# A ninth column in the first heads' inverse root, and k's second half sent from ScalarE's queue

## The chip, the cores and the metric

One NeuronCore of a Trainium2 chip runs the whole program once. The metric is the device time of that execution in microseconds (us); lower is better. The core has five engines that run side by side, each with its own in-order instruction stream: TensorE (PE: matmuls; its weight loads are shown as PEld), VectorE (DVE), ScalarE (ACT), GpSimd (POOL) and SyncE (SP), which here only starts transfers. ScalarE can start transfers too; a transfer is then an instruction of its stream, and it waits there for its data like any other.

## The reference, cut to what matters

Two transformer layers over 512 tokens of width 1024. Layer 0 mixes with eight dilated-window heads (A) and eight sliding-window heads (B), layer 1 with sixteen forgetting-attention heads (C); each layer ends in a squared-ReLU MLP. What the change touches is at the start of layer 0 and in every head:

```
h = rms_norm(x, g_mix)                  # per token: x * rsqrt(mean(x*x) + EPS) * g
proj = h @ w_in
q = rms_norm(q per head, q_gain)        # per token and head of 64 columns
k = rms_norm(k per head, k_gain)
scores = q @ k.T * scale + bias         # then softmax, times v
```

## The kernel before, in words

Tokens lie in four tiles of 128. The projections run on the transposed input, multiplied by the gain but not yet by the tokens' inverse root. That root is put in afterwards: v is multiplied by it when it leaves PSUM (`rcol`, one column per token tile, in `prep_v`), and for q and k, which are normed per head anyway, only its EPS term is needed (`ecol`, added in `norm_heads`). Every matrix product is made of three fp32r products (high x high, low x high, high x low), so each weight tile `wraw` is split into `whi` (ScalarE or GpSimd) and `wlo` (VectorE or GpSimd), and each activation into a high and a low half.

`start` does the first projection (q and k of the first four A heads, `pj`) while its inputs arrive: for each of eight chunks of 128 input columns it splits the input chunk (`h`, high on ScalarE, low on VectorE) and the weight chunk, and issues twelve matmuls. Between chunks it squares the tokens (`junk`, `ms`, chunks 3 to 6) and makes tables for the attention biases. After chunk 6 it calls `col_stats`: two small operations give `msv` and `ecol`, and eleven dependent ones in `rsqrt_small` (a shift, a subtraction and three Newton rounds of three) give `rcol`. In `start` these are held in program order, ahead of chunk 7's low halves. Then `use(outs)` calls `norm_heads`: copies of `pj` to `qk` and squares on ScalarE, sums `ss` on VectorE, `ssv`, the same eleven operations over 32 columns (8 heads in 4 tiles), and four multiplications of `qk`, two on VectorE and two on GpSimd.

Next comes the v projection of these heads (`v_a(0)`), then attention, interleaved with further projections as filler for TensorE. Per pair of heads `prep_q` and `prep_k` transpose `qk` on TensorE, split it, and `prep_k` copies the 64 partitions of each k to the other 64 by a transfer from SBUF to SBUF (256 KB in reads and writes, 26 of them in all), since the score matmul takes high and low from both halves. Weight and bias loads share SyncE's queue with these transfers, in program order.

Outside the places held in program order, a scheduler fixes the order on each engine when the program is built. PSUM has four banks in `pA` (projections) and four in `pB` (transposes, scores, outputs); the v projection may write a bank only when the q,k projection in it was copied out, and the next projection (k and v of B, `kv_b`) only when `prep_v` has read v.

Of the kernel before, what the change touches and what calls it, by code (L numbers as in the profile page):

```python
# [9 lines left out]
F32 = mybir.dt.float32  # L10
F32R = mybir.dt.float32r
BF16 = mybir.dt.bfloat16
I32 = mybir.dt.int32
AF = mybir.ActivationFunctionType
OP = mybir.AluOpType
# [3 lines left out]
P = 128  # L19
# [50 lines left out]
def trunk(ctx, tc, x, b_sinks, w_out_even, b_forget, w_out_odd, w_up, w_down, xt, gains, w_in_even, w_in_odd, out):  # L70
# [46 lines left out]

    cnt = {"hi": 0, "start": False}

    def rsqrt_small(dst, v):  # L120

        n = v.shape[2]
        y, t1 = (small.tile([P, NT * 8], F32, tag=f"rsq{i}", name="rsq")[:, :NT * n]
                 .rearrange("p (t h) -> p t h", h=n) for i in range(2))
        b = small.tile([P, NT * 8], I32, tag="rsqb", name="rsqb")[:, :NT * n].rearrange("p (t h) -> p t h", h=n)
        in_order(nc.vector.tensor_scalar(b, v.bitcast(I32), 1, None, op0=OP.logical_shift_right))
        in_order(nc.vector.tensor_scalar(y.bitcast(I32), b, -1.0, float(0x5f3759df), op0=OP.mult, op1=OP.add))
        for k in range(3):
            in_order(nc.vector.scalar_tensor_tensor(t1, v, -0.5, y, op0=OP.mult, op1=OP.mult))
            in_order(nc.vector.tensor_mul(t1, t1, y))  # L130
            in_order(nc.vector.scalar_tensor_tensor(dst if k == 2 else y, t1, 1.5, y, op0=OP.add, op1=OP.mult))
# [8 lines left out]
    def in_order(m):  # L140
        if cnt["start"]:
            tc.keep_in_program_order(m)
# [50 lines left out]
    def layer_attention(li, hT, w_in, w_out, stats=None):  # L193


        with ExitStack() as c2:
# [39 lines left out]
                use(outs)  # L236
                yield 0

            def norm_heads(outs, nh, sq_tag="sq", sq_bufs=1 + li):

                w = nh * HD
                qk = [ap.tile([P, 2, 512], F32, tag="qk", bufs=4, name="qk") for _ in range(2)]
                ss = small.tile([P, NT, 8], F32, tag="ss", name="ss")
                for t in range(NT):
                    nc.scalar.copy(qk[t // 2][:, t % 2, :w], outs[t][:, :w])
                for t in range(NT):
                    q = qk[t // 2][:, t % 2, :w]
                    sq = ap.tile([P, 512], F32, tag=sq_tag, bufs=sq_bufs, name="sq")
                    nc.scalar.activation(sq[:, :w], q, AF.Square)
                    nc.vector.reduce_sum(ss[:, t, :nh], sq[:, :w].rearrange("p (h d) -> p h d", d=HD), axis=AX.X)  # L250
                v = small.tile([P, NT, 8], F32, tag="ssv", name="ssv")
                for t in range(NT):
                    nc.vector.tensor_scalar(v[:, t, :nh], ss[:, t, :nh], 1.0 / HD, ecol[:, t:t + 1],
                                            op0=OP.mult, op1=OP.add)
                rs = small.tile([P, NT, 8], F32, tag="rs", name="rs")
                rsqrt_small(rs[:, :, :nh], v[:, :, :nh])
                for t in range(NT):
                    q = qk[t // 2][:, t % 2, :w].rearrange("p (h d) -> p h d", d=HD)
                    eng = nc.gpsimd if NORM[t] == "g" else nc.vector
                    eng.tensor_mul(q, q, rs[:, t, :nh].unsqueeze(2).to_broadcast([P, nh, HD]))  # L260
                return qk

            def head_T(qk, off):
# [17 lines left out]
            def prep_k(qk, off, g):  # L281

                pt = head_T(qk, off)
                ks = []
                for h in range(2):
                    k = ap.tile([P, 2, 512], F32R, tag="K", bufs=3, name="K")
                    r = slice(h * HD, (h + 1) * HD)
                    r2 = slice((1 - h) * HD, (2 - h) * HD)
                    scale_split(k[r, 0], k[r, 1], pt[r], g[r])
                    nc.sync.dma_start(k[r2].bitcast(F32), k[r].bitcast(F32))  # L290
                    ks.append(k)
                return ks

# [204 lines left out]
                return use  # L498

            def qk_use(key, nh, *sq):  # L500
                def use(outs):
                    st["qk", key] = norm_heads(outs, nh, *sq)
                return use

            def all_of(gen):
# [91 lines left out]
    def start(ap, hT, w_in, tables, outs, use):  # L597

        w = bank("pB", "warm")
        for _ in range(WARM):
            nc.tensor.matmul(w[:, :P], identb, identb, start=True, stop=True)

        cnt["start"] = True
        xs = [ap.tile([P, 2, 512], F32, tag="qk", bufs=4, name="xs") for _ in range(4)]
        raws = [wp.tile([P, 2, 512], F32, tag="wraw", bufs=RAW, name="wraw") for _ in range(4)]
        tok = [acc_slot(f"x{i}") for i in range(4)]

        def load(what, k, n):  # L610
            if what == "t":
                dst = tok[k]
                src = x[0, k % 2 * 256:k % 2 * 256 + 256, k // 2 * 512:k // 2 * 512 + 512]
            else:
                dst = (xs if what == "x" else raws)[k // 2][:, k % 2:k % 2 + n]
                src = (xt if what == "x" else w_in[:, :512])[k * P:(k + n) * P]
            in_order(nc.sync.dma_start(dst, src.rearrange("(c p) t -> p c t", p=P)))

        for what, k, n in (("x", 0, 1), ("w", 0, 1), ("x", 1, 1), ("w", 1, 1), ("x", 2, 2), ("w", 2, 2), ("t", 0, 0), ("x", 4, 2),
                           ("t", 1, 0), ("w", 4, 2), ("t", 2, 0), ("x", 6, 2), ("t", 3, 0), ("w", 6, 2)):  # L620
            load(what, k, n)
        ms = small.tile([P, 2, NT], F32, tag="ms0", name="ms0")
        sink = small.tile([P, HA], F32, tag="sink", name="sink")
        for _ in range(TABLES0):
            next(tables)
        for k in range(DC):
            g = gcol[:, k:k + 1]
            src = xs[k // 2][:, k % 2]
            h = slot(f"h0_{k}")
            hT.append(h)  # L630
            hi = wp.tile([P, 512], F32R, tag="whi", bufs=NHI, name="whi")
            lo = wp.tile([P, 512], F32R, tag="wlo", bufs=NLO, name="wlo")
            raw = raws[k // 2][:, k % 2]
            if k == 0:
                in_order(nc.scalar.activation(h[:, 0, :256], src[:, :256], AF.Copy, scale=g))
                in_order(nc.scalar.copy(hi, raw))
                in_order(nc.scalar.activation(h[:, 0, 256:], src[:, 256:], AF.Copy, scale=g))
                in_order(nc.vector.tensor_sub(lo, raw, hi.bitcast(F32)))
                in_order(nc.vector.scalar_tensor_tensor(h[:, 1], src, g, h[:, 0].bitcast(F32), op0=OP.mult, op1=OP.subtract))
            else:  # L640
                scale_split(h[:, 0], h[:, 1], src, g)
                split(hi, lo, raw, "act")
            products = ((0, hi), (0, lo), (1, hi))
            for n, (t, i) in enumerate([(t, i) for i in range(3) for t in range(NT)] if k == 0 else
                                       [(t, i) for t in range(NT) for i in range(3)]):
                part, wt = products[i]
                m = nc.tensor.matmul(outs[t], h[:, part, t * P:(t + 1) * P], wt, start=k == 0 and i == 0,
                                     stop=k == DC - 1 and i == 2)
                if k == 0:
                    in_order(m)  # L650
            for _ in range(TABLES[k]):
                next(tables)
            if k == 1:
                in_order(nc.scalar.dma_start(sink, bass.AP(tensor=b_sinks.tensor, offset=b_sinks.offset, ap=[[0, P], [1, HA]])))
                in_order(nc.scalar.dma_start(bfor, bass.AP(tensor=b_forget.tensor, offset=b_forget.offset, ap=[[0, P], [1, HC]])))
            if 3 <= k < 7:
                i = k - 3
                for t in range(2):
                    junk = ap.tile([P, 512], F32, tag="sq", bufs=1, name="junk")
                    in_order(nc.scalar.activation(junk, tok[i][:, t], AF.Square,  # L660
                                                  accum_out=ms[:, i // 2, i % 2 * 2 + t:i % 2 * 2 + t + 1]))
            if k == 6:
                in_order(nc.vector.tensor_add(ms[:, 0], ms[:, 0], ms[:, 1]))
                col_stats(ms[:, 0])
        cnt["start"] = False
        nc.gpsimd.tensor_scalar(nsink, sink, -1.0, 1.0, op0=OP.mult, op1=OP.mult)
        tc.keep_in_program_order(nc.vector.tensor_mul(gg, gcol[:, 32:38:2], gcol[:, 33:38:2]))
        use(outs)
        for _ in tables:
            pass  # L670

# [586 lines left out]
```

## Time and profile before

| what | us |
|---|---|
| median of 3 runs (1164.63 to 1164.91) | 1164.66 |
| the profiled execution | 1165.4 |
| its span | 1163.6 |
| TensorE busy in the span | 1144.3 |
| VectorE / ScalarE / GpSimd busy | 875.7 / 646.4 / 201.1 |

The profiled execution's time lies 1.8 us above its span and 0.7 us above the median. Of the 1163.6 us, TensorE is not busy in 19.3; where it is busy without a break, a stage is as long as its matmuls. In lists of waits the columns are: who waited and on which line, for whom, us in total, times, longest. In the timeline: start, duration, engine, line, operation, and in brackets the idle time before it with what ended it.

### The profile page before, as it was taken

To read this page: it belongs to the slowest core of one execution; us is meant where nothing else is said; L and a number is where in the kernel's file an instruction comes from. 1 tells how busy PE (TensorE), PEld (TensorE's weight loads), DVE (VectorE), ACT (ScalarE), POOL (GpSimd) and SP (SyncE) were. 2 spreads that over 40 slices of the span, in tenths; PEclk is the share of its full clock that TensorE was granted. 3 is DMA by queue.
4 is the path that set the end of the run, shared out by engine and by line. 5 is a ranking of instruction groups with operands and counts; after the bars stand their busy time and mean duration, and the time that the engine had idled before them with its cause. 6 is when DMAs were issued, how large, how long until landed. Compare 5 with 4: busy or idle time off the path is not lost.

```text
span 1163.6 us, 17370 instructions
## 1 busy us (share of the span) xinstructions
PE 1144.3 (98%) x6228; PEld 979.7 (84%) x6228; DVE 875.7 (75%) x1875; ACT 646.4 (56%) x1342; POOL 201.1 (17%) x292
## 2 busy tenths in 40 slices
PE   8999999999999999999999999999999999999998
PEld 6887887888988988988887888888888888888887
DVE  7877999968868857855646877778858759669676
ACT  6455867656545545444235685656756455465452
POOL 0345534100000000000255445332100000000000
PEclk9999999999999999999999999999999999999999
DMA  7432124142332333333443323343420721623403
GB/s 272 145 83 81 37 50 150 56 127 88 95 109 91 93 107 92 108 111 110 146 128 109 110 84 108 101 131 114 164 99 8 233 86 56 198 73 110 146 35 109
DMA packets 94694, 126.56 MB, mean 109 GB/s; under 512 B 5888, under 2 KB 66304, under 8 KB 94608
## 3 DMA queue, kind: packets, MB, share of 16 engines
q1 hardware_dynamic: 93568, 123.29, 34.4%
q10 hardware_dynamic: 1040, 2.16, 0.5%
q8 instruction: 49, 0.80, 0.3%
q14 instruction: 37, 0.30, 0.1%
HBM read 114.39 MB, written 4.23 MB: 102 GB/s over the span
## 4 chain that ended last, share of the span: by engine, by line
PE 87%; DVE 5%; DMA 3%; ACT 2%; issue 1%; POOL 1%; SPq 0%; POOLq 0%; DVEq 0%; ACTq 0%
PE up L161 10%; PE up L165 10%; PE up L164 10%; PE pj L232 4%; PE pj L230 4%; PE pj L231 4%; PE O L382 3%; PE PT L362 3%; PE op L165 2%; PE op L161 2%; PE op L164 2%; PE Y L1019 2%; PE Y L1018 2%; PE Y L1016 2%; PE S L325 2%; PE Y L1065 1%
## 5 line engine op out<-in xcount | busy, mean ns | idle before, releaser
L161 PE MATMUL up<-xin,whi 128*128 128x512 f32 x512 | 200.5, 392 | 0.0
L165 PE MATMUL up<-xin,whi 128*128 128x512 f32 x512 | 199.3, 389 | 0.0
L164 PE MATMUL up<-xin,wlo 128*128 128x512 f32 x512 | 199.2, 389 | 0.0
L765 ACT CAST whi<-wraw 128x512 fp32r<-128x512 f32 x228 | 139.2, 619 | 105.0 <-PE up L165 47.7
L766 DVE TENSOR_TENSOR wlo<-wraw,whi 128x512 fp32r<-128x512 f32 x228 | 151.7, 685 | 50.9 <-ACT whi L765 50.7
L165 PEld LDWEIGHTS up<-xin,whi 128*128 128x128 f32 x512 | 96.1, 188 | 20.1
L164 PEld LDWEIGHTS up<-xin,wlo 128*128 128x128 f32 x512 | 96.2, 188 | 19.8 <-issue 0.2
L161 PEld LDWEIGHTS up<-xin,whi 128*128 128x128 f32 x512 | 96.2, 188 | 19.7 <-issue 0.2
L342 ACT ACTIVATE P<-P,negm 128x128 f32<-128x128 f32 (+5 forms) x128 | 69.5, 543 | 45.1 <-DVE negm L339 43.2
L149 POOL TENSOR_SCALAR whi<-wraw 128x512 fp32r<-128x512 f32 x88 | 60.2, 686 | 166.7 <-PE pj L232 119.9
L947 ACT ACTIVATE u<-up 128x512 f32<-128x512 f32 x64 | 38.3, 599 | 90.9 <-PE up L165 90.9
L230 PE MATMUL pj<-whi,hn 128*128 128x512 f32 (+2 forms) x256 | 88.7, 347 | 0.0
L232 PE MATMUL pj<-whi,hn 128*128 128x512 f32 (+2 forms) x256 | 86.9, 339 | 0.0
L231 PE MATMUL pj<-wlo,hn 128*128 128x512 f32 (+2 forms) x256 | 86.8, 339 | 0.0
L786 DVE TENSOR_TENSOR t<-u 128x256 f32<-128x256 f32 x56 | 23.2, 423 | 62.8 <-ACT u L1090 61.1
L152 POOL TENSOR_TENSOR wlo<-wraw,whi 128x512 fp32r<-128x512 f32 x48 | 64.4, 1345 | 21.2 <-ACT whi L147 18.7
L350 POOL TENSOR_SCALAR P<-P,rden 128x256 f32<-128x256 f32 (+2 forms) x96 | 48.9, 512 | 81.2 <-DVE rden L345 75.9
L152 DVE TENSOR_TENSOR wlo<-wraw,whi 128x512 fp32r<-128x512 f32 (+1 forms) x71 | 49.2, 701 | 18.2 <-POOL whi L149 14.3
L374 ACT CAST PT<-PT 128x256 fp32r<-128x256 f32 (+3 forms) x128 | 49.1, 403 | 21.6 <-PE PT L362 20.7
L339 DVE CUSTOM_DVE_ANT_0 P<-S,bias 128x128 f32<-128x128 f32 (+1 forms) x96 | 45.7, 484 | 17.7 <-PE S L328 12.2
L765 ACT CAST whi<-mraw 128x512 fp32r<-128x512 f32 x64 | 38.8, 619 | 33.1 <-DVE mraw L876 14.4
L230 PE MATMUL pj<-whi,h 128*128 128x256 f32 (+1 forms) x160 | 54.3, 340 | 1.1 <-DVE v L157 1.1
(231 smaller groups left out, 3091.5 us busy)
## 6 DMA issues: line engine op xcount, KB each, us to landing
wraw<-in_w_up SPq DMA_DIRECT2D x64, 512.0 KB, 4.2
wraw<-in_w_down SPq DMA_DIRECT2D x56, 512.0 KB, 3.8
wraw<-in_w_in_odd SPq DMA_DIRECT2D x22, 512.0 KB, 3.8
wraw<-in_w_in_even SPq DMA_DIRECT2D x17, 512.0 KB, 5.3
mraw<-in_w_down SPq DMA_DIRECT2D x16, 512.0 KB, 4.7
K<-K SPq DMA_DIRECT2D x26, 256.0 KB, 2.9
bias<-csp SPq DMA_DIRECT2D x16, 256.0 KB, 3.3
wraw<-in_w_out_odd SPq DMA_DIRECT2D x8, 512.0 KB, 3.6
```

The costliest lines, as they stand in the source:

```text
L149: nc.gpsimd.tensor_scalar(dst_h, src, 1.0, 1.0, op0=OP.mult, op1=OP.mult)
L152: in_order((nc.gpsimd if lo == "pool" else nc.vector).tensor_sub(dst_l, src, dst_h.bitcast(F32)))
L161: m = nc.tensor.matmul(o, wh, xh, start=start, stop=False, skip_group_check=more)
L164: nc.tensor.matmul(o, wl, xh, start=False, stop=False, skip_group_check=more)
L165: nc.tensor.matmul(o, wh, xl, start=False, stop=stop, skip_group_check=more)
L230: nc.tensor.matmul(o, xh, hi[:, :n], start=k == 0, stop=False)
L231: nc.tensor.matmul(o, xh, lo[:, :n], start=False, stop=False)
L232: nc.tensor.matmul(o, xl, hi[:, :n], start=False, stop=k == DC - 1)
L342: nc.scalar.activation(p[:, :ne], p[:, :ne], AF.Exp, scale=-1.0, bias=negm[:, i:i + 1], accum_out=den[:, i:i + 1])
L374: nc.scalar.copy(dst[:, 0], pt[:, :n])
L765: sca(nc.scalar.copy(dst_h, src))
L766: late.append(lambda: vec(nc.vector.tensor_sub(dst_l, src, dst_h.bitcast(F32))))
```

## The change

The sum of the token squares stays in `start`, but `col_stats` is not called there any more. The mean squares go to `norm_heads` through `use(outs, ms[:, 0])`. With them given, `norm_heads` makes its working tiles nine columns wide in a scratch tile (`room`, in the place of `sq`), puts the tokens' mean square + EPS in the ninth, makes `ecol` from it, runs the eleven operations once over 36 columns, multiplies `qk`, and copies the ninth column to `rcol`. The other calls of `norm_heads` and layer 1's `col_stats` are as before. And in `prep_k` the transfer is issued from ScalarE's stream.

```
-    def rsqrt_small(dst, v):
+    def rsqrt_small(dst, v, room=None):
         n = v.shape[2]
+        if room:
+            y, t1, b = room[2:]
+            b = b.bitcast(I32)
+        else: ...
...
+                    room = ap.tile([P, 512], F32, tag=sq_tag, bufs=sq_bufs, name="room")
...
+                    v, rs = room[:2]
+                    nc.vector.tensor_scalar(v[:, :, nh], ms, 1.0 / D, EPS, op0=OP.mult, op1=OP.add)
+                    nc.vector.tensor_scalar_mul(ecol, v[:, :, nh], EPS)
                 for t in range(NT):
                     nc.vector.tensor_scalar(v[:, t, :nh], ss[:, t, :nh], 1.0 / HD, ecol[:, t:t + 1],
                                             op0=OP.mult, op1=OP.add)
-                rsqrt_small(rs[:, :, :nh], v[:, :, :nh])
+                rsqrt_small(rs, v, room)
...
+                if ms is not None:
+                    nc.vector.tensor_copy(rcol, rs[:, :, nh])
...
-                    nc.sync.dma_start(k[r2].bitcast(F32), k[r].bitcast(F32))
+                    nc.scalar.dma_start(k[r2].bitcast(F32), k[r].bitcast(F32))
...
-            if k == 6:
-                in_order(nc.vector.tensor_add(ms[:, 0], ms[:, 0], ms[:, 1]))
-                col_stats(ms[:, 0])
         cnt["start"] = False
+        nc.vector.tensor_add(ms[:, 0], ms[:, 0], ms[:, 1])
...
-        use(outs)
+        use(outs, ms[:, 0])
```

VectorE's order at the end of `start`, before, from the last Newton round on (`h_7` is the low half of chunk 7's input, the `wlo` behind it that of its weights):

```order
L129 SCALAR_TENSOR_TENSOR rsq<-msv,rsq 128x4
L130 TENSOR_TENSOR rsq<-rsq 128x4
L131 SCALAR_TENSOR_TENSOR rcol<-rsq 128x4
L157 SCALAR_TENSOR_TENSOR h_7_359<-xs,gcol,h_7_359 128x512
L152 TENSOR_TENSOR wlo<-wraw,whi 128x512
L667 TENSOR_TENSOR gg<-gcol 128x3
L152 TENSOR_TENSOR wlo<-wraw,whi 128x512 x6
```

And now, from the sum of the token squares on:

```order
L679 TENSOR_TENSOR ms_168<-ms_168 128x4
L681 TENSOR_TENSOR gg<-gcol 128x3
L721 TENSOR_SCALAR f<-dist 128x256
L322 SCALAR_TENSOR_TENSOR bias<-dist,lt 128x512
L161 SCALAR_TENSOR_TENSOR h_7_341<-xs,gcol,h_7_341 128x512
L156 TENSOR_TENSOR wlo<-wraw,whi 128x512
L725 TENSOR_TENSOR lb<-lb,f 128x256
L156 TENSOR_TENSOR wlo<-wraw,whi 128x512 x5
L322 SCALAR_TENSOR_TENSOR bias<-dist,lt 128x512
L156 TENSOR_TENSOR wlo<-wraw,whi 128x512
```

The thirteen small operations are gone from ahead of chunk 7's low halves; one table (`lb`) and one bias stand behind them instead of ahead.

VectorE at the end of the first heads' chain, before (`rs` is the result, `pj_427` to `pj_430` are the v projection's banks):

```order
L130 TENSOR_TENSOR rsq<-rsq 128x32
L131 SCALAR_TENSOR_TENSOR rs<-rsq 128x32
L260 TENSOR_TENSOR qk<-qk,rs 128x512 x2
L157 SCALAR_TENSOR_TENSOR v_103<-pj_427,rcol,v_103 128x4x64
L157 SCALAR_TENSOR_TENSOR v_103<-pj_428,rcol,v_103 128x4x64
L157 SCALAR_TENSOR_TENSOR v_103<-pj_429,rcol,v_103 128x4x64
L152 TENSOR_TENSOR wlo<-wraw,whi 128x512
L157 SCALAR_TENSOR_TENSOR v_103<-pj_430,rcol,v_103 128x4x64
```

And now, first how the chain opens, then how it ends (the Newton rounds between are those of before over 36 columns):

```order
L265 TENSOR_SCALAR room<-ms_168 128x4
L266 TENSOR_SCALAR ecol<-room 128x4
L268 TENSOR_SCALAR room<-ss,ecol 128x8 x4
L130 TENSOR_SCALAR room<-room 128x36
L131 TENSOR_SCALAR room<-room 128x36
```

```order
L135 SCALAR_TENSOR_TENSOR room<-room 128x36
L274 TENSOR_TENSOR qk<-qk,room 128x512 x2
L276 COPY rcol<-room 128x4
L161 SCALAR_TENSOR_TENSOR v_103<-pj_409,rcol,v_103 128x4x64
L161 SCALAR_TENSOR_TENSOR v_103<-pj_410,rcol,v_103 128x4x64
L161 SCALAR_TENSOR_TENSOR v_103<-pj_411,rcol,v_103 128x4x64
L156 TENSOR_TENSOR wlo<-wraw,whi 128x512
L161 SCALAR_TENSOR_TENSOR v_103<-pj_412,rcol,v_103 128x4x64
```

The order around the v rows is as it was, but `rcol`, which ScalarE's high halves of v need as well, is now written behind the multiplications of `qk`.

ScalarE at the first pair of heads, before:

```order
L277 CAST Q<-qkT 64x512
L156 ACTIVATE K<-qkT,gg 64x512
L277 CAST Q<-qkT 64x512
L156 ACTIVATE K<-qkT,gg 64x512
L342 ACTIVATE P,den<-P,negm 128x128
```

And now:

```order
L293 CAST Q<-qkT 64x512
L160 ACTIVATE K<-qkT,gg 64x512
L293 CAST Q<-qkT 64x512
L306 DMA K<-K 64x1024
L160 ACTIVATE K<-qkT,gg 64x512
L306 DMA K<-K 64x1024
L358 ACTIVATE P,den<-P,negm 128x128
```

Two transfers stand in ScalarE's stream, each behind VectorE's low half of the same k; the second k's high half now stands behind the first transfer. All 13 pairs look like this but that in some another operation stands between. In SyncE's stream the weight and bias loads close up. From the first pair on, the scheduler also interleaves attention and projection matmuls of layer 0 differently in places; their number is the same.

More of the change, by code (lines that the diff above doesn't have):

```diff
@@ L118, in trunk @@
     cnt = {"hi": 0, "start": False}
-    def rsqrt_small(dst, v):
+    def rsqrt_small(dst, v, room=None):
         n = v.shape[2]
-        y, t1 = (small.tile([P, NT * 8], F32, tag=f"rsq{i}", name="rsq")[:, :NT * n]
-                 .rearrange("p (t h) -> p t h", h=n) for i in range(2))
-        b = small.tile([P, NT * 8], I32, tag="rsqb", name="rsqb")[:, :NT * n].rearrange("p (t h) -> p t h", h=n)
+        if room:
+            y, t1, b = room[2:]
+            b = b.bitcast(I32)
+        else:
+            y, t1 = (small.tile([P, NT * 8], F32, tag=f"rsq{i}", name="rsq")[:, :NT * n]
+                     .rearrange("p (t h) -> p t h", h=n) for i in range(2))
+            b = small.tile([P, NT * 8], I32, tag="rsqb", name="rsqb")[:, :NT * n].rearrange("p (t h) -> p t h", h=n)
         in_order(nc.vector.tensor_scalar(b, v.bitcast(I32), 1, None, op0=OP.logical_shift_right))
@@ L237, in project, with norm_heads @@
                 yield 0
-            def norm_heads(outs, nh, sq_tag="sq", sq_bufs=1 + li):
+            def norm_heads(outs, nh, sq_tag="sq", sq_bufs=1 + li, ms=None):
                 w = nh * HD
@@ L250, in norm_heads @@
                     nc.vector.reduce_sum(ss[:, t, :nh], sq[:, :w].rearrange("p (h d) -> p h d", d=HD), axis=AX.X)
-                v = small.tile([P, NT, 8], F32, tag="ssv", name="ssv")
+                if ms is None:
+                    v = small.tile([P, NT, 8], F32, tag="ssv", name="ssv")[:, :, :nh]
+                    rs = small.tile([P, NT, 8], F32, tag="rs", name="rs")[:, :, :nh]
+                    room = None
+                else:
+                    room = ap.tile([P, 512], F32, tag=sq_tag, bufs=sq_bufs, name="room")
+                    room = [room[:, i * NT * (nh + 1):(i + 1) * NT * (nh + 1)]
+                            .rearrange("p (t h) -> p t h", h=nh + 1) for i in range(5)]
+                    v, rs = room[:2]
+                    nc.vector.tensor_scalar(v[:, :, nh], ms, 1.0 / D, EPS, op0=OP.mult, op1=OP.add)
+                    nc.vector.tensor_scalar_mul(ecol, v[:, :, nh], EPS)
                 for t in range(NT):
@@ L254, in norm_heads @@
                                             op0=OP.mult, op1=OP.add)
-                rs = small.tile([P, NT, 8], F32, tag="rs", name="rs")
-                rsqrt_small(rs[:, :, :nh], v[:, :, :nh])
+                rsqrt_small(rs, v, room)
                 for t in range(NT):
@@ L500, in qk_use, with use @@
             def qk_use(key, nh, *sq):
-                def use(outs):
-                    st["qk", key] = norm_heads(outs, nh, *sq)
+                def use(outs, ms=None):
+                    st["qk", key] = norm_heads(outs, nh, *sq, ms=ms)
                 return use
```

## The prediction

> **What bounds the kernel now.** I read the page's engine rows first, then TensorE's waits, then busy time by stage, then the timeline of the two places that the waits name.
>
> ```profile
> PE 1144.3 (98%) x6228; PEld 979.7 (84%) x6228; DVE 875.7 (75%) x1875; ACT 646.4 (56%) x1342; POOL 201.1 (17%) x292
> ```
>
> TensorE is the bound with 98%; at most 19.3 us of idle time, and whatever the clock loses, can be won. Its waits (who on which line, for whom: total us, times, longest):
>
> ```profile
> PE pj L647 <- DVE wlo L152: 3.0, 2, 2.7
> PE S L325 <- DMA K<-K: 2.3, 2, 1.6
> PE pj L230 <- DVE v L157: 1.1, 1, 1.1
> PE qkT L267 <- POOL qk L260: 1.0, 2, 0.5
> ```
>
> The first is the largest that a kernel could avoid, and stands where the change removes work; the second is the only one that ends in a transfer of k; the third is the v rows' wait, where the change adds one. By stage (TensorE's busy time is the second number of a row, its granted clock the third from the end):
>
> ```profile
> 28.00:30.00 2.00, 0.00 (x0) 0.00 (x0) 1.90 (x8) 1.11 (x3) 0.00 (x0) 1.00 0.00 0
> 31.00:32.00 1.00, 1.00 (x5) 0.78 (x4) 1.00 (x3) 0.97 (x3) 0.00 (x0) 0.73 0.79 119
> 32.00:33.00 1.00, 1.00 (x4) 0.74 (x3) 1.00 (x2) 0.82 (x3) 0.00 (x0) 0.50 1.01 358
> 34.00:35.00 1.00, 1.00 (x7) 1.00 (x7) 0.51 (x2) 0.91 (x2) 0.00 (x0) 0.56 0.82 240
> 60.00:220.00 160.00, 154.34 (x887) 129.37 (x886) 139.56 (x404) 104.74 (x281) 72.51 (x125) 1.00 0.27 80
> 600.00:815.00 215.00, 212.61 (x1289) 181.66 (x1288) 165.67 (x448) 132.44 (x314) 93.25 (x121) 1.00 0.37 108
> ```
>
> TensorE stands still before 30 us and then gets half its clock from about 31.5 to 34.9: of the four us from 31 to 35 (33 to 34 taken like its neighbour) it loses 0.27 + 0.5 + 0.5 + 0.44 = 1.7 us. So the wait costs 2.75 + 1.7, nearly 4.5 us. Attention in layer 0 after 60 us has 5.7 us of idle time in small pieces, in layer 1 2.4 us, nearly all of it the wait for k.
>
> **Chunk 7, removed.** VectorE, ScalarE and TensorE around it:
>
> ```profile
> 24.91 0.16 DVE L663 TENSOR_TENSOR ms<-ms 128x4 f32<-128x4 f32 x1 [0.35 <-ACT junk L660]
> 25.26 0.69 DVE L306 SCALAR_TENSOR_TENSOR bias<-dist,lt 128x512 f32<-128x512 f16 x1
> 28.66 0.74 DVE L157 SCALAR_TENSOR_TENSOR h<-xs,gcol,h 128x512 fp32r<-128x512 f32 x1
> 29.32 0.68 DVE L152 TENSOR_TENSOR wlo<-wraw,whi 128x512 fp32r<-128x512 f32 x1
> 29.99 3.69 DVE L152 TENSOR_TENSOR wlo<-wraw,whi 128x512 fp32r<-128x512 f32 x6
> 25.39 3.72 ACT L147 CAST whi<-wraw 128x512 fp32r<-128x512 f32 x7
> 26.70 0.61 PE L647 MATMUL pj<-whi,h 128*128 128x512 f32 x2
> 30.05 0.50 PE L647 MATMUL pj<-wlo,h 128*128 128x512 f32 x1 [2.75 <-DVE wlo L152]
> 33.77 0.41 PE L230 MATMUL pj<-whi,h 128*128 128x256 f32 x1
> ```
>
> In the new order `ms`, `gg`, one table and one bias come first: 24.91 + 0.08 + 0.08 + 0.2 + 0.6 = 25.87 (occupancies from start to start). Then the low half of chunk 7's input, 0.66, and `wlo` from 26.53 to 27.21 (its `whi` is the first of the seven casts, ready at 26.0). TensorE, which wanted it at about 27.2, waits 0.1 instead of 2.75, and the slow clock behind the gap goes. The remaining eleven matmuls at 0.23 end at 29.8, and v's projection starts there instead of 33.77: 4.0 us won so far. Not all stays: ScalarE's seven casts hold it to 29.11 and the v projection's four banks free up only as the copies of `pj` come out, four copies and a square at 0.52 to 0.6, so the fourth at 31.9. The first twelve v matmuls end at 32.3 instead of 35.7, and the lead is 3.4.
>
> **The ninth column, moved.** The rows that set the end of this stage are the norm chain's and v's:
>
> ```profile
> 33.60 0.67 DVE L250 TENSOR_REDUCE ss<-sq 128x8 f32<-128x512 f32 x1
> 38.59 0.68 DVE L250 TENSOR_REDUCE ss<-sq 128x8 f32<-128x512 f32 x1
> 39.58 0.18 DVE L126 TENSOR_SCALAR rsqb<-ssv 128x32 int32<-128x32 int32 x1
> 41.21 1.17 DVE L130 TENSOR_TENSOR rsq<-rsq 128x32 f32<-128x32 f32 x1
> 43.32 2.14 DVE L260 TENSOR_TENSOR qk<-qk,rs 128x512 f32<-128x512 f32 x2
> 45.39 1.26 DVE L157 SCALAR_TENSOR_TENSOR v<-pj,rcol,v 128x256 fp32r<-128x256 f32 x3
> 46.99 1.10 DVE L152 TENSOR_TENSOR wlo<-wraw,whi 128x512 fp32r<-128x512 f32 x1 [0.35 <-POOL whi L149]
> 40.99 1.34 POOL L152 TENSOR_TENSOR wlo<-wraw,whi 128x512 fp32r<-128x512 f32 x1
> 43.42 2.95 POOL L260 TENSOR_TENSOR qk<-qk,rs 128x512 f32<-128x512 f32 x2 [1.09 <-issue]
> 45.97 0.48 ACT L156 ACTIVATE v<-pj,rcol 128x256 fp32r<-128x256 f32 x1 [0.96 <-PE pj L232]
> 45.91 0.38 PE L230 MATMUL pj<-whi,h 128*128 128x256 f32 x1
> 48.54 0.39 PE L230 MATMUL pj<-whi,h 128*128 128x256 f32 x1 [1.11 <-DVE v L157]
> ```
>
> Before, TensorE ended v's projection at 45.9 and met v's first bank freed at the same moment: the chain was as late as the matmuls. Now: seven `wlo` low halves, a table and a bias hold VectorE to 31.73 (27.13 + 0.34 + 0.6 + 6 x 0.61), so the first sum starts 1.9 us earlier. Square and sum take turns on one `sq` tile; from first to last sum took 4.99 with two waits for TensorE of 0.7 and 0.6, of which little is left: about 4.2, the last sum at 35.9, 2.7 earlier. Behind it stand two dependent operations (0.2 each) and the four sums' `ssv` (0.5 instead of one at 0.27): the chain opens at 37.55 instead of 39.58, 2.0 earlier. The extra four columns cost nothing that the rows show (0.16 for 4 columns, 0.18 for 32). The eleven operations took 3.74 against eleven at 0.22, since GpSimd's split ran beside them (the row of 1.17 ends where GpSimd's `wlo` ends, at 42.33). That split waits for TensorE's v projection and comes as much earlier, so I keep 3.74: `rs` at 41.3, again 2.0 earlier.
>
> Here the price is paid. Before, ScalarE's four high halves of v ran as each bank came ready, under the chain. Now they need `rcol`: 41.3 + 2.07 for the products + 0.15 for the copy, then 0.5 on ScalarE and 0.45 on VectorE: the first bank is free at 44.6, while TensorE is through at 42.45 (32.3 + 84 x 0.12). A wait of 2.1 us for v replaces that for `wlo`. The fourth bank, behind the `wlo` that waits for GpSimd, comes at 46.9 instead of 48.5. So at this point 1.6 us are won of the 4.0. Bounds: 0.5 if the opening is slower or the clock drops again (next part); 3.1 if the 1.3 us lost beside GpSimd go and everything behind follows.
>
> **K's transfer, moved to ScalarE.** 26 issues leave SyncE and enter ScalarE.
>
> ```profile
> L290 SPq DMA_DIRECT2D K<-K x26: 461/467/522, 51.6 to 789.8; - x26
> DMA to landing us min/median/max: 2.8/2.9/4.9
> 620.80 2.01 SPq L290 DMA_DIRECT2D K<-K  x2
> 624.76 0.36 PE L325 MATMUL S<-K,Q 128*128 128x256 f32 x1 [1.61 <-DMA K<-K]
> 6.76 0.46 ACTq L655 DMA_DIRECT2D bfor<-in_b_forget  x1
> 78.66 0.40 ACT L342 ACTIVATE P<-P,negm 128x128 f32<-128x128 f32 x1 [3.18 <-DVE negm L339]
> 769.23 0.40 ACT L342 ACTIVATE P<-P,negm 128x128 f32<-128x128 f32 x1 [1.67 <-DVE negm L339]
> ```
>
> On ScalarE an issue costs about 0.47 (its own row of 0.46 agrees), and it waits for VectorE's low half, with the second high half or the first exponential behind it: 26 x 0.47 = 12.2 us of issue, and per pair the second wait of about 0.7. Both lie in the pause between the k casts and the first exponential (3.2 us in the row at 78.66, 1.7 at 769.23), so I take nothing on the path. The second k comes 0.5 later, before its scores are due. What can be won is the wait for k: issued at 620.80 and used at 624.76, 3.96 against a median landing of 2.9. Bounds: none (both queues carry the same bytes beside the same weight load), or 1.06 twice, cut by the 0.7 of the smaller wait: 1.7. I take 0.3, near the first, because the issue is not earlier. SyncE's loads no longer stand behind k's, but no TensorE wait of the list ends in a weight load there: nothing.
>
> [...] No run so far shows a k transfer issued from ScalarE.
>
> **The other interleaving.** Layer 0 after 60 us has 5.7 us of idle time that a new order can shift either way; bounds -2 and +2, taken as 0.
>
> **The sum.** -1.6 - 0.3 + 0 = -1.9 against the execution of 1165.4 (span 1163.6), hence 1163.5 there; from the median of 1164.66 it gives 1162.8. I put 0.4 back for the half of a clock drop (below) that the likeliest case may still hold: **1163.2**. A difference below 0.2%, 2.3 us, counts as no change.
>
> **Rivals.** (1) *The clock drops behind the new wait.* 2.75 us of standing still cost 1.7 us of clock; the 1.6 at 624.76 cost none (clock 1.00 in its stage). A wait of 2.1 lies between. If it counts, half clock for 3.4 us takes 0.8 (part falls into the wait for the fourth bank) to 1.7: 1163.6 to 1164.5. [...] Chance 0.22.
>
> (2) *The lead is kept.* If GpSimd's split falls beside another stretch, the chain is 1.3 shorter, v comes at 43.3 and 3 us are won here; with k's 0.3 to 1: 1161.0. For it: the 1.17 row is one accident of overlap. Against: both sides move together. Chance 0.20.
>
> (3) *Slower: ScalarE blocks.* With the issue and the wait in ScalarE's stream, the exponentials or `PT` casts behind come late and TensorE waits for them in most of the 13 pairs. Each issue pair plus wait is 0.94 + 0.7 = 1.6 us; where half of it shows, 0.8 x 13 = 10; where a third does in half the pairs, 3.5. It decides against the change from 0.33 us a pair on (4.2 in all, which takes back 1.9 and adds 2.3). A typical loss would be 5, so 1168. Against it: the pauses quoted. Chance 0.11.
>
> (4) *The wait at chunk 7 stays* for another reason (a weight load or a cast that only now shows): 1164.7. The `whi` there was ready 3 us early, so 0.05.
>
> **Numbers.** The forecast has 0.42, and its own spread is 1162.3 to 1164.2. Under 1162.3: (2) and a quarter of the forecast, 0.30. Over 1167.0: (3) without its mild end, 0.10. Between: 0.60. Range 1160.8 to 1166.8.
>
> **What the profile would show.** Right: no `wlo` wait at 27 to 30 us, clock 1.00 from 31 to 35; a TensorE wait of about 2 us for VectorE's v between 42 and 45; K's issues on ScalarE with 0.47 each, its landing still near 2.9; the waits for k in layer 1 within 0.5 of before. Wrong: a row of slow clock between 43 and 50, waits of TensorE for ScalarE's exponentials, or idle time in 60 to 220 us off 5.7 by more than 2.

## The result, and the profile after

The change made the kernel slower: 1168.16 us median of six executions (1165.03 to 1169.45) against 1164.64 beside them, ratio 1.0025 [1.0014, 1.0036]. A second measurement gave 1166.33 (1165.43 to 1168.55) against 1164.40, ratio 1.0019 [1.0010, 1.0029]. (The ratios compare all executions; the quotients of the medians are 1.0030 and 1.0017.) Forecast was 1163.2 in a range from 1160.8 to 1166.8. The profiled execution has a span of 1166.7, 3.1 more than the one shown of before.

Of the page of the change, the row of TensorE, then three rows of its waits:

```profile
PE 1146.4 (98%) x6228; PEld 981.2 (84%) x6228; DVE 874.2 (75%) x1865; ACT 646.8 (55%) x1342; POOL 201.4 (17%) x292
```

```profile
PE pj L234 <- DVE v L161: 4.4, 2, 3.5
PE S L341 <- DVE Q L294: 1.7, 1, 1.7
PE S L341 <- DMA K<-K: 1.4, 2, 1.2
```

The wait for `wlo` at chunk 7 is gone. The wait for v, 1.1 before, is now 4.4; a wait for q of 1.7 is new; the waits for k went from 2.3 to 1.4. TensorE is busy 2.1 us longer with the same 6228 matmuls, so it ran slower. Its busy time (second number) and granted clock (third from the end) in stages that were shown of before:

```profile
32.00:33.00 1.00, 1.00 (x10) 1.00 (x10) 0.21 (x1) 0.87 (x2) 0.00 (x0) 1.00 1.07 377
34.00:35.00 1.00, 1.00 (x11) 1.00 (x10) 0.90 (x3) 0.75 (x3) 0.00 (x0) 1.00 0.67 256
60.00:220.00 160.00, 154.43 (x890) 130.09 (x889) 139.40 (x409) 106.71 (x285) 71.64 (x125) 0.99 0.27 80
600.00:815.00 215.00, 212.41 (x1286) 180.79 (x1284) 162.39 (x445) 132.19 (x312) 94.19 (x123) 1.00 0.37 108
```

The slow clock behind chunk 7 is gone as forecast, and the idle time of 60 to 220 (5.6 us, 5.7 before) and of 600 to 815 (2.6, 2.4 before) is nearly the same. What is lost lies between 41 and 54 and near 108. The timeline there, VectorE, ScalarE, GpSimd and TensorE:

```profile
36.29 0.50 DVE L265 TENSOR_SCALAR room<-ms 128x4 f32<-128x4 f32 x1
37.02 1.55 DVE L268 TENSOR_SCALAR room<-ss,ecol 128x8 f32<-128x8 f32 x4
38.61 0.18 DVE L130 TENSOR_SCALAR room<-room 128x36 int32<-128x36 int32 x1
41.12 2.14 DVE L274 TENSOR_TENSOR qk<-qk,room 128x512 f32<-128x512 f32 x2
43.18 1.00 DVE L276 COPY rcol<-room 128x4 f32<-128x4 f32 x1
44.79 1.27 DVE L161 SCALAR_TENSOR_TENSOR v<-pj,rcol,v 128x256 fp32r<-128x256 f32 x3 [0.60 <-ACT v L160]
44.28 1.57 ACT L160 ACTIVATE v<-pj,rcol 128x256 fp32r<-128x256 f32 x4 [8.75 <-DVE rcol L276]
36.14 0.62 POOL L153 TENSOR_SCALAR whi<-wraw 128x512 fp32r<-128x512 f32 x1 [22.55 <-PE pj L236]
36.84 1.30 POOL L156 TENSOR_TENSOR wlo<-wraw,whi 128x512 fp32r<-128x512 f32 x1
41.22 2.95 POOL L274 TENSOR_TENSOR qk<-qk,room 128x512 f32<-128x512 f32 x2 [3.07 <-issue]
45.33 0.39 PE L234 MATMUL pj<-whi,h 128*128 128x256 f32 x1 [3.52 <-DVE v L161]
47.70 0.58 PE L234 MATMUL pj<-whi,h 128*128 128x256 f32 x1 [0.86 <-DVE v L161]
```

`rs` is there at 41.1. The copy to `rcol` stands behind the multiplications of `qk` and takes 1.00 for four columns: it ends at 44.18, when GpSimd's multiplications end (41.22 + 2.95 = 44.17). ScalarE, idle for 8.75, can only then begin v's high halves; the first bank is free at 45.3, while v's last matmul started at 41.53.

TensorE's clock behind that wait, in stretches chosen so that the switches fall on their borders, first of the change, then of before:

```profile
40.18:43.60 3.42, 1.63 (x14) 1.43 (x12) 3.27 (x7) 0.00 (x0) 2.38 (x2) 1.00 0.00 0
43.60:47.01 3.41, 1.51 (x10) 1.28 (x10) 2.81 (x5) 1.57 (x4) 3.02 (x4) 1.00 0.00 0
47.01:50.42 3.41, 2.72 (x12) 2.72 (x13) 1.06 (x3) 0.76 (x2) 0.00 (x0) 0.50 0.54 152
50.42:53.84 3.42, 3.42 (x17) 3.42 (x17) 2.03 (x4) 1.76 (x3) 0.62 (x1) 0.50 0.29 62
105.04:108.45 3.41, 1.79 (x8) 0.89 (x7) 2.85 (x3) 0.15 (x1) 3.41 (x3) 1.00 0.67 211
108.45:111.86 3.41, 3.41 (x11) 2.80 (x10) 0.81 (x2) 1.16 (x2) 1.45 (x2) 0.50 0.36 77
```

```profile
28.05:31.47 3.42, 1.42 (x6) 1.18 (x7) 3.32 (x10) 1.67 (x5) 0.00 (x0) 1.00 0.14 15
31.47:34.88 3.41, 3.41 (x13) 2.83 (x12) 3.04 (x6) 2.46 (x5) 0.00 (x0) 0.50 0.89 267
621.97:625.38 3.41, 1.80 (x11) 1.25 (x9) 1.05 (x3) 0.83 (x1) 0.00 (x0) 1.00 0.92 220
```

The clock is at half for 6.83 us from 47.01 and for 3.41 from 108.45: (2.72 + 3.42 + 3.41)/2 = 4.8 us of TensorE's work lost, against 1.7 before. The difference, 3.1, is as large as that of the spans, in part by chance: of those 3.1, TensorE's busy time makes 2.1 and its idle time 1.0. Ahead of each drop to half clock in these rows stands a stretch of 3.41 us in which TensorE was busy for 1.51, 1.79 or 1.42 us; the second half-clock stretch of the change, from 50.42, stands behind one with 2.72 at half clock.

Executions also begin differently (chunk 7's first matmul starts at 25.59 to 26.92), so landmarks are counted from chunk 7's first matmul (us after it; TensorE's starts in the traces):

| execution | chunk 7 | v begins | k, v of B begins | its fourth bank | first scores | first `up` | last `up` |
|---|---|---|---|---|---|---|---|
| before | 26.92 | 6.85 | 18.99 | 21.62 | 27.9 | 201.1 | 1093.5 |
| before, again | 25.81 | 6.81 | 18.96 | 21.57 | 27.8 | 201.2 | 1093.1 |
| the change | 26.27 | 3.02 | 19.06 | 21.43 | 30.4 | 204.6 | 1097.3 |
| the change, again | 26.09 | 2.94 | 19.03 | 21.39 | 28.2 | 202.7 | 1094.5 |
| ninth column alone | 25.86 | 2.96 | 19.01 | 21.37 | 28.3 | 202.7 | 1094.6 |
| ninth column, copy first | 25.59 | 3.08 | 17.58 | 20.20 | 28.0 | 201.4 | 1093.2 |

The 3.8 us won at v's beginning are gone, to the last tenth, at the first bank of the next projection. From there to the first `up` the first execution of the change falls 3.5 behind and the second 1.5; half clock takes 4.8 and 3.4 of their work where neither execution of before has any there, and some of that is hidden by later waits, which are not taken apart here.

### The profile page after: what moved, and what is told of

Same layout as the page of the kernel before. It is cut to its first block, busy times and chain, and to the rows that moved or that the text cites. A ratio compares the mean times of both kernels' runs of the same rounds, so it can differ in the third digit from the quotient of the medians.

```text
span 1166.7 us, 17371 instructions
## 1 busy us (share of the span) xinstructions
PE 1146.4 (98%) x6228; PEld 981.2 (84%) x6228; DVE 874.2 (75%) x1865; ACT 646.8 (55%) x1342; POOL 201.4 (17%) x292
## 4 chain that ended last, share of the span: by engine, by line
PE 80%; DVE 3%; ACT 1%; POOL 0%; issue 0%; DMA 0%; POOLq 0%
PE up L165 10%; PE up L168 10%; PE up L169 10%; PE pj L234 3%; PE pj L236 3%; PE pj L235 3%; PE op L169 2%; PE op L165 2%; PE op L168 2%; PE O L398 2%; PE PT L378 2%; PE Y L1032 2%; PE Y L1030 2%; PE Y L1033 2%; PE Y L1079 1%; PE Y L1082 1%
## 5 line engine op out<-in xcount | busy, mean ns | idle before, releaser
L779 ACT CAST whi<-mraw 128x512 fp32r<-128x512 f32 x64 | 38.8, 620 | 33.1 <-DVE mraw L890 14.4
```

What stands on the lines that cost most here:

```text
L779: sca(nc.scalar.copy(dst_h, src))
```

## The experiments

Beside each ratio stands its 95% interval; medians are over 11 executions unless said otherwise.

**The two halves apart.** TensorE's matmuls stand in the order of before with the ninth column alone; all of the other interleaving comes with k's transfers on ScalarE.

```
(of the change)  -nc.scalar.dma_start(k[r2]...)   +nc.sync.dma_start(k[r2]...)
```

> The ninth column as changed, k's transfers back on SyncE's queue (TensorE's order of matmuls is then that of before). Theory A (rcol comes only behind the multiplications of qk, TensorE stands still about 3.5 us at the end of v's projection, and half clock follows): the loss stays, 1166 to 1169.5, with a wait for VectorE's v of 3 to 4 us and granted clock 0.5 for 3.4 or 6.8 us behind it. Theory B (ScalarE's issues and the other interleaving make the loss): 1162 to 1164, faster than before by 1 to 2.5, since the wait at chunk 7 is gone.

```
(of before)      -nc.sync.dma_start(k[r2]...)     +nc.scalar.dma_start(k[r2]...)
```

> Only k's transfers moved to ScalarE's queue; the token's inverse root as before, ahead of chunk 7. Theory A: within 1.5 of before (1163.2 to 1166.2), the wait of 2.75 at chunk 7 unchanged, no wait of TensorE for ScalarE's exponentials over 0.5. Theory B: the loss of the change shows here, 1167 to 1170.

Ninth column alone: 1165.45, 1.0013 [1.0004, 1.0022]; mean granted clock over its executions 0.9968, that of before 0.9988. A little under the lower end that theory A gave, and on its side. The wait (timeline) and the slow clock (stretches) are those of the change:

```profile
44.87 0.38 PE L234 MATMUL pj<-whi,h 128*128 128x256 f32 x1 [3.51 <-DVE v L161]
```

```profile
41.97:45.38 3.41, 0.51 (x4) 0.51 (x5) 2.81 (x5) 1.55 (x4) 3.33 (x5) 1.00 0.00 0
45.38:48.80 3.42, 3.23 (x15) 2.85 (x15) 1.80 (x3) 0.01 (x1) 0.86 (x1) 0.50 0.25 44
```

k alone: 1165.17, 1.0011 [1.0002, 1.0019]: within the 1.5 us of theory A, but not nothing.

**The thirteen small operations later, without a ninth column.**

```
             if k == 6:
-                in_order(nc.vector.tensor_add(ms[:, 0], ms[:, 0], ms[:, 1]))
-                col_stats(ms[:, 0])
         cnt["start"] = False
+        nc.vector.tensor_add(ms[:, 0], ms[:, 0], ms[:, 1])
+        col_stats(ms[:, 0])
```

> No ninth column; the thirteen small operations for ecol and rcol as before, but no longer held ahead of chunk 7's low halves: they stand among them and behind. k's transfers on SyncE. Theory A: chunk 7's wait goes as in the change, and ScalarE's high halves of v run under the norm chain as before; VectorE's low halves still stand behind two multiplications of qk, so the first v bank comes near 44 and TensorE waits 1.5 to 2.5 instead of 3.5: 1161 to 1164, half clock behind it in some executions only. Rival (what counts is that the norm chain ends near 41 and v's low halves come behind the multiplications, whenever rcol is there): first bank near 45 and 1166 to 1169 as in the change.

1164.24, 1.0002 [0.9993, 1.0011], just above the range of theory A. ScalarE's high halves ran early, and the wait was in between:

```profile
43.46 0.39 PE L230 MATMUL pj<-whi,h 128*128 128x256 f32 x1 [1.84 <-DVE v L157]
46.07 0.49 PE L230 MATMUL pj<-whi,h 128*128 128x256 f32 x1 [1.10 <-DVE v L157]
```

So the ninth column isn't needed to take the wait at chunk 7 away, and taking it away gains nothing yet. The mean granted clock over its executions is 0.9972, that of before 0.9988; the difference, 0.0016 of 1164 us, is worth 1.9 us by estimate and may be where the gain went, which was not tried.

**The copy to `rcol` first.** This moves one instruction; TensorE's order is unchanged, with k on SyncE (that of before) and with k on ScalarE (that of the change).

```
                 rsqrt_small(rs, v, room)
+                if ms is not None:
+                    nc.vector.tensor_copy(rcol, rs[:, :, nh])
                 for t in range(NT):
                     ...  eng.tensor_mul(q, q, rs...)
-                if ms is not None:
-                    nc.vector.tensor_copy(rcol, rs[:, :, nh])
```

> As the run with the ninth column alone (k's transfers on SyncE; TensorE's order is that of before), but the copy of the ninth column to rcol stands ahead of the multiplications of qk, not behind. Theory A (rcol's place in VectorE's stream sets how long TensorE stands still): ScalarE's high halves run beside the multiplications, the first v bank comes at about 43.4 instead of 44.9, the wait is 2.0 instead of 3.5, and half clock follows in fewer executions: 1163.5 to 1164.8, mean granted clock 0.9975 instead of 0.9968. Rival (VectorE and GpSimd together take until 44 whatever stands first): wait of 3 or more, 1165 to 1166.

> The change as it is, k's transfers on ScalarE, but the copy to rcol ahead of the multiplications of qk instead of behind (TensorE's order is that of the change). If the two halves of the change only add up: the run with copy first and k on SyncE (ratio 0.9994 to before) plus the cost of k alone (1.0011) gives 1.0005, about 1164.5, some 2.3 less than the change (1.0025), with a wait of 1.7 instead of 3.5 for the first v bank. Rival (the other interleaving that comes with k on ScalarE makes the loss together with the late start): 1.002 or more.

With k on SyncE 1163.69, 0.9994 [0.9985, 1.0003]; with k on ScalarE 1165.37, 1.0005 [0.9996, 1.0014]. VectorE, ScalarE and TensorE of the first in the timeline, then TensorE's clock by stretches:

```profile
40.51 0.17 DVE L272 COPY rcol<-room 128x4 f32<-128x4 f32 x1
40.58 2.14 DVE L276 TENSOR_TENSOR qk<-qk,room 128x512 f32<-128x512 f32 x2
42.65 1.25 DVE L161 SCALAR_TENSOR_TENSOR v<-pj,rcol,v 128x256 fp32r<-128x256 f32 x3
40.77 1.57 ACT L160 ACTIVATE v<-pj,rcol 128x256 fp32r<-128x256 f32 x4 [5.96 <-PE pj L236]
43.17 0.39 PE L234 MATMUL pj<-whi,h 128*128 128x256 f32 x1 [1.69 <-DVE v L161]
```

```profile
42.72:46.13 3.41, 1.86 (x13) 1.63 (x13) 2.67 (x6) 0.00 (x0) 3.33 (x4) 1.00 0.00 0
46.13:49.55 3.42, 3.42 (x19) 3.42 (x18) 1.44 (x3) 1.85 (x4) 0.34 (x1) 0.50 0.50 153
```

The copy takes 0.17 here, ScalarE's work lies under the multiplications, and v's low halves follow them at once. The step from 1.0013 to 0.9994, and that from 1.0025 and 1.0019 to 1.0005, have the same size, 1.4 to 2.0 thousandths: 1.6 to 2.3 us for the place of one copy. The theory's numbers held; that the sum of the parts (1.0005) came out to the last digit is luck, with intervals of 0.0009 to either side. With k on ScalarE most of the step is the wait and not the clock: the waits for v are 2.3 in all instead of 3.5 in the change's second profile, while the mean granted clock is 0.9969 with the copy first and 0.9966 in the eleven executions of the change, and both profiles have two half-clock stretches (from 43.93 and 105.37 with the copy first, from 45.32 and 106.76 in the change). With k on SyncE the clock moves too, from 0.9968 to 0.9982.

**Matmuls in the waits.** They write a bank that nothing reads; the waits themselves stay. After `all_of(v_a(0))`, 13 of them in the change and 7 with copy first; behind chunk 6's matmuls, 11 in the kernel before:

```
+                wm = bank("pB", "warm2")
+                for n in range(13):
+                    nc.tensor.matmul(wm, hT[n % 8][:, 0, :P], hT[n % 8][:, 0], start=True, stop=True)
```

> The change, with 13 matmuls more (128x512, their result is not used) between v's projection and the next one, where TensorE stood still 3.5 us: 13 x 0.23 = 3.0 us of work that nothing waits for. Theory A with the clock following idle time: the next projection still starts near 45.3, but with granted clock 1.00 from 45 to 54, so about 3 us less than the change: 1164 to 1166.5. Rival (the slow clock has another cause, or the wait itself is all of the loss): 0.5 again behind 47, 1167.5 to 1169.

> Copy first, k on SyncE, and 7 matmuls more (128x512, result not used, 7 x 0.23 = 1.6 us) in the wait of 1.7 for the first v bank. If half clock behind that wait is what is left of the loss there: mean granted clock 0.999 instead of 0.9983, 1162.2 to 1163.2. Rival (the clock's loss is hidden by the next waits): within 0.4 of the run with copy first (ratio 0.9994).

> The kernel before, with 11 matmuls more (128x512, result not used, 11 x 0.23 = 2.5 us) in the wait of 2.75 at chunk 7. The wait stays, the half clock behind it (3.4 us, 1.7 lost in the executions that have it) goes: mean granted clock 1.000 instead of 0.9988, 1 to 1.7 faster than before if that clock costs at the end, nothing if v's first bank, which waits for the norm chain, sets the end anyway (theory: about 0.3, since TensorE met that bank just as it came free).

The change, filled: 1165.85, 1.0012 [1.0003, 1.0021]; mean granted clock 0.9988, where the change had 0.9958 in its first six executions and 0.9966 in the eleven later ones. The k, v projection starts where it did, at full clock (timeline, then the clock behind it). Further on, near 150, its profile has a half-clock stretch, behind one with the wait for q in it (the last two rows):

```profile
45.29 0.39 PE L235 MATMUL pj<-whi,h 128*128 128x256 f32 x1 [0.26 <-DVE v L162]
```

```profile
45.30:54.00 8.70, 7.73 (x62) 7.52 (x63) 5.88 (x9) 2.95 (x6) 2.34 (x3) 1.00 0.41 101
148.93:152.34 3.41, 1.76 (x12) 1.54 (x12) 3.20 (x9) 1.21 (x4) 0.45 (x2) 1.00 0.62 162
152.34:155.75 3.41, 3.41 (x18) 3.38 (x17) 3.00 (x16) 2.05 (x7) 1.48 (x5) 0.50 0.43 150
```

So with the wait filled the clock behind it stays at 1.00, where the two profiles of the change have 0.50: here the clock goes with TensorE's idle time. That this costs the change 0.7 to 1.3 thousandths is the middle of intervals that overlap. With copy first, filling gains nothing that can be measured: 1163.59, 0.9995 [0.9987, 1.0004], at a mean clock of 0.9994. And before, filled, isn't faster either: 1165.43, 1.0007 [0.9999, 1.0016]. The wait only moves:

```profile
28.94 0.50 PE L647 MATMUL pj<-wlo,h 128*128 128x512 f32 x1 [0.22 <-DVE wlo L152]
44.28 0.39 PE L230 MATMUL pj<-whi,h 128*128 128x256 f32 x1 [1.04 <-DVE v L157]
```

In this execution the clock is full from end to end (1.000), and its 1164.69 is no less than before's median of 1164.23. But over its eleven executions the mean granted clock is 0.9988, not the 1.000 expected and practically that of before, 0.9987: in eight of them it is 0.998 or 0.999, so slow somewhere. Only three ran at 1.000, at 1163.91 to 1164.69. So no gain is seen from the 1.7 us of slow clock at chunk 7; that it cost the kernel before nothing at its end rests on these three alone.

**v first.** From the kernel with the small operations later: v's low halves, held in order, ahead of the multiplications of `qk`, VectorE's low half of the first weight tile that GpSimd casts behind them, and `LEADS[0]` from 0.0 to 0.08, which puts 12 more matmuls ahead of the first transposes.

```
+                vg = v_a(0)
+                ...                      # its matmuls
+                cnt["start"] = True      # program order: v's halves, then qk * rs
+                all_of(vg)
+                for f in later: f()
+                cnt["start"] = False
```

> No ninth column: the token's inverse root as before but among chunk 7's low halves, not ahead of them; the four low halves of v are put ahead of the first heads' multiplications of qk on VectorE, GpSimd's first weight split behind them, and 12 more matmuls of the k, v projection ahead of the first transposes. k's transfers on SyncE. Theory A: v's first bank is free when TensorE comes to it at about 41.7, no wait over 0.5 there, granted clock 1.00 from 40 to 60, and the 4 us won at chunk 7 stay: 1159.5 to 1161.5. Rival (the first pair of heads comes late instead, TensorE waits for qk, q or k): waits of 1.5 or more between 43 and 60, 1162.5 to 1164.

> The same with k's transfers issued from ScalarE's queue. If the move of the transfers costs by itself (the run with that move alone was 1.2 slower): 0.8 to 1.6 more than the run with v first. Rival (what cost there was the other order of layer 0's matmuls, which is another again here): anything from 1 less to 2 more, with the difference in TensorE's waits between 100 and 230, none of them for a transfer or an exponential. Rival (no cost): within 0.4.

1164.97 (12 executions), 1.0008 [0.9998, 1.0018]; with k on ScalarE 1167.13 (5 executions), 1.0031 [1.0019, 1.0043]. Theory A failed, and the rival's waits between 43 and 60 did not come either; with k on ScalarE the loss is above all three expectations. From 40 to 60 all is as theory A said, and the lead is lost behind that (stretches, then timeline):

```profile
40.00:60.00 20.00, 20.00 (x152) 19.13 (x151) 16.18 (x54) 11.50 (x35) 10.01 (x15) 1.00 0.13 27
60.00:65.00 5.00, 3.56 (x18) 2.41 (x17) 4.86 (x16) 1.80 (x5) 3.33 (x4) 1.00 0.00 0
75.70:79.12 3.42, 1.11 (x8) 0.75 (x7) 0.90 (x2) 0.00 (x0) 0.62 (x1) 1.00 0.69 165
79.12:82.53 3.41, 3.41 (x14) 3.02 (x13) 2.28 (x10) 2.57 (x9) 0.67 (x2) 0.50 0.27 91
```

```profile
64.39 0.50 PE L236 MATMUL pj<-wlo,h 128*128 128x512 f32 x1 [1.00 <-DVE wlo L152]
78.40 0.36 PE L337 MATMUL S<-K,Q 128*128 128x256 f32 x1 [2.31 <-DMA K<-K]
```

TensorE has its first scores at 50.0, 3.6 before the second profile of before, and then waits for a weight's low half on VectorE and for k, with two half-clock stretches (from 79.12 and 106.43). (GpSimd's own three low halves take 4.71 from 62.48 on; VectorE's two beside them take 2.88 from 64.85 on, one of VectorE's at 71.12 takes 0.69.) Even its four executions at a granted clock of 1.000 took 1163.1 to 1163.9. So a lead of nearly 4 us at the start is taken up in the attention stage. The run changes four things at once, the interleaving by `LEADS[0]` among them; which of them loses the lead was not told apart.

**k's transfers, layer by layer, and the two kernels again.**

```
(of before)  -nc.sync.dma_start(k[r2]...)  +(nc.scalar if li else nc.sync).dma_start(k[r2]...)
(of before)  -nc.sync.dma_start(k[r2]...)  +(nc.sync if li else nc.scalar).dma_start(k[r2]...)
```

> The kernel before with only layer 1's sixteen k transfers issued from ScalarE; layer 0, and its interleaving, as before. If the cost of k on ScalarE (1.2 us with all 26) lies in the issue itself: 16 of 26 of it, about 0.7. If it lies in layer 0's other interleaving: within 0.3 of before. A gain is possible too, if the waits for k in layer 1 shrink.

> The kernel before with only layer 0's ten k transfers issued from ScalarE, and so with layer 0's other interleaving; layer 1's sixteen on SyncE. If k's cost (ratio 1.0011 with all 26) comes with layer 0's interleaving: 1.0008 to 1.0014, with a lower mean granted clock than before (0.998 instead of 0.9988), since the new wait of 1.7 for q near 150 is followed by half clock in some executions. If it comes from the issues one by one: 10 of 26 of it, 1.0004. If the first measurement of k alone was chance: within 0.0005 of before.

> The kernel before, for a second profile. The profiled execution shown of it (1165.4) is near the upper end of its 33 runs on this chip (1163.0 to 1165.5). Expected: a span near 1162.2, the wait for k at 624 nearer 1.0 than 1.61, and the slow clock at chunk 7 in place or not, as the stretch of TensorE's pause falls.

> The change itself once more, for more executions and a second profile. If its loss is the late first v bank and the clock behind it: 1.002 to 1.003 again, a wait of 3.5 for v in the same place, half clock behind it of 3.4 or 6.8 us wherever the grid of stretches falls, and no half clock at 108 in most executions.

Layer 1 alone: 1164.48, 1.0001 [0.9992, 1.0010]. Layer 0 alone, with the other interleaving and its wait of 1.7 for q: 1164.26, 1.0000 [0.9992, 1.0009]. Neither theory of a cost is borne out, though neither interval shuts out what it gave: the parts show nothing, the whole gave 1.0011, and the pairs with k on either queue (1.0005 less 0.9994; 1.0031 less 1.0008) 1.1 and 2.3 thousandths more. What k's move costs, between nothing and some 2.7 us, and where, stays open; no run shows a gain. From ScalarE k lands no sooner (transfer, queue, KB, median us to landing; layer 1's sixteen, each from one of the two runs):

```profile
K<-K ACTq DMA_DIRECT2D x16, 256.0 KB, 3.4
```

```profile
K<-K SPq DMA_DIRECT2D x16, 256.0 KB, 2.9
```

Before, again: span 1162.1, slow clock behind chunk 7, waits for k 1.5 in all. The execution shown of before was thus 1.1 late at chunk 7 and 0.8 at k. The change, again, is given above: its waits for k are 2.3 in all, as many as in the execution shown of before; the wait of 3.52 for v is the same, half clock followed for 3.41 us at 45.32 and, against what was expected, again at 106.76:

```profile
41.91:45.32 3.41, 0.20 (x1) 0.20 (x2) 2.81 (x4) 1.25 (x4) 3.33 (x5) 1.00 0.00 0
45.32:48.74 3.42, 3.40 (x16) 3.02 (x16) 2.11 (x4) 0.32 (x1) 1.16 (x1) 0.50 0.17 22
103.35:106.76 3.41, 1.86 (x8) 1.12 (x9) 2.53 (x3) 0.32 (x1) 3.33 (x4) 1.00 0.58 198
```

## Why the prediction was wrong, step by step

Times in this section up to the clock are counted, as in the table, from chunk 7's first matmul: forecasts from before's 26.92, on which they were worked out, measured ones from the change's 26.27.

*Chunk 7, removed: right.* The wait is gone, v's projection begins at 3.0 (2.9 forecast) and its matmuls end at 15.5, as forecast.

*The chain opens 2.0 earlier: wrong.* The last sum starts at 9.3 (9.0 forecast), but the chain opens at 12.3 instead of 10.6, since `room`'s first operation and the four `ssv` took 0.50 and 1.55 where I put 0.2 and 0.5. I had kept GpSimd's split beside the eleven operations, because "both sides move together". They did not: the split came 3.5 earlier, more than the chain did, and ran beside these operations (`whi` from 36.14 to 36.76, `wlo` from 36.84); the eleven operations took 2.5, not 3.74. The two errors nearly cancel: `rs` at 14.8, 14.4 forecast.

*The price of the late `rcol`: the step that failed.* I put 0.15 for the copy, from its size; it took 1.00 behind the multiplications, up to the end of GpSimd's. v's first bank came at 19.1 instead of 17.7, the fourth at 21.4 instead of 20.0, where before had 19.0 and 21.6, and TensorE stood still for 3.52 + 0.86 instead of 2.1. Of the 1.4 at the first bank the copy makes 0.85 and the later `rs` 0.5. (As written, the terms for that bank add up to 44.5 us of the trace, not 44.6.) Of "1.6 us won" 0.2 is left.

*The clock: rival 1 was what happened, at twice its size.* I gave it 0.22 and at most 1.7, from the one row of 3.4 us. Here half clock lasted two stretches, the first of them with the wait of 0.86 in it (2.72 busy): 3.1 lost behind v, and 1.7 more at 108. Asking whether a pause of 2.1 counts was the wrong question. The switches of the change lie at 47.01, 53.84, 108.45 and 111.86: 6.83, 54.61 and 3.41 apart, 2, 16 and 1 times 3.413 (54.61/16). So in this execution the four switches lie on one grid of such stretches, and how busy TensorE is within one goes with what follows. In the rows shown, shares of 0.06 to 0.55 (0.20 to 1.86 of 3.41) at full clock were followed by half clock; 1.63 at 40.18 and 1.80 at 621.97 were not, so near one half the share alone does not decide. Where the grid lies against the program differs by execution: the first drop comes 20.74 after chunk 7's first matmul in one profile of the change and 19.23 in the other, and the difference of 1.51 is no multiple of 3.41. So the same wait may be cheap in one and dear in the next: of the change with the copy first, three executions at a granted clock of 0.994 or 0.995 took 1166.39 to 1166.62, three at 0.999 took 1163.01 to 1165.00. The wait at 624.76, which I took as a sign that 1.6 us cost none, was one draw.

*k on ScalarE: sign not borne out.* Forecast -0.3; measured alone 1.0011, in parts nothing. The waits for k in the profile did shrink by 0.9, but before's second profile shows 1.5 without the change, and the change's second profile 2.3 with it: that was the execution, not the queue. Of the two bounds of the forecast for this part, none and 1.7, the first was nearer.

*The other interleaving.* Idle time in layer 0 stayed within 0.1 of 5.7, as taken; that it belonged wholly to k's move and not to the ninth column I hadn't separated. *The slower rival* had the right side and the wrong mechanism: TensorE's list has no wait for an exponential, and 0.5 in one wait for a `PT` cast. *A lead that is kept* (rival 2) was wrong twice: the lead was lost at v, and the kernel that kept it lost it by 80 us.

## What to carry to other kernels

Before pricing a wait that is removed, find the next point where another engine's chain arrives at the same moment, and count only what is won there: with v first, nearly 4 us won at the start gave nothing that could be measured at the end. When a small result is moved behind larger work, price the queue position and the engines running beside it, not the instruction: one copy of four columns cost 1.6 to 2.3 us by its place, and a change that wants the ninth column should put it ahead of the multiplications. A wait that moved to another place was no even exchange for TensorE's clock here (4.8 us of work lost against 1.7): count the busy share in any 3.4 us around the new wait (half clock followed shares up to 0.55), and compare kernels over many executions.

## What was not expected of the hardware

The clock's grid, above. And small VectorE operations beside GpSimd's large ones took several times as long here: 1.00 for the copy that takes 0.17 ahead of them. Two `ssv` operations of the run with the small operations later, the second beside GpSimd's weight split:

```profile
32.88 0.23 DVE L253 TENSOR_SCALAR ssv<-ss,ecol 128x8 f32<-128x8 f32 x1
36.02 0.57 DVE L253 TENSOR_SCALAR ssv<-ss,ecol 128x8 f32<-128x8 f32 x1
```

Each of the long ones ends with GpSimd's operation, to 0.03 us: the copy at 44.18 and GpSimd's multiplications at 44.17, `room`'s first operation at 36.79 and `whi` at 36.76, this `ssv` at 36.59 and that run's `whi` at 36.57. The profile shows the overlap and the common end; why was not tried.

No version here is shown to beat the kernel before: copy first with k on SyncE (0.9994 [0.9985, 1.0003]) comes nearest, and it does beat the change, whose intervals lie above its own.
